# A bias table built by eight matmuls instead of one, an ordering edge in the last block, and two groups side by side in a decoder layer

## The chip, the cores and the metric

The kernel runs on one core of one Trainium2 chip. The metric is the time of one execution on the device in microseconds (us), as the median of several runs. Beside the runs there is one execution taken by the hardware profiler; its span is the time from its first to its last instruction. In the rows of the profile PE is the matrix engine (PEld its weight loads), DVE the vector engine, ACT the scalar engine, POOL the GpSimd engine and SP the engine whose queue starts nearly all transfers; a q behind a name (SPq, ACTq) is that engine's queue of instructions. L430 is line 430 of the kernel.

## The reference

One decoder layer over 2048 positions of width 1024, in float32:

```python
h = rmsnorm(x, norm1[l])
q, k, v, b_gate, c_gate, hc, p = jnp.split(h @ w_in[l], splits, axis=-1)
attn_out = sliding_window_attention(q, k, v, sinks[l], rel_bias)   # 8 heads, window 128
conv_out = short_conv_mixer(b_gate, c_gate, hc, conv_w[l])
pool_out = multiscale_pool_mixer(p, pool_w[l], pool_scale[l])
x = x + jnp.concatenate([attn_out, conv_out, pool_out], -1) @ w_out[l]
x = x + jnp.square(jax.nn.relu(rmsnorm(x, norm2[l]) @ w1[l])) @ w2[l]
return rmsnorm(x, final_norm)
```

In the attention each block of 128 queries sees 256 keys, and to each score a bias is added that depends on the distance between query and key (through 32 buckets) and on the head; outside the window the score is -1e30. For one head the bias of a block is therefore a matrix of 128 by 256 whose rows are one row of 384 values, shifted by one place from row to row.

## The kernel before

Every float32 operand is split into a high part (a cast to the matrix engine's fp32r) and a low part (the rest), and a product is three matmuls of 128 x 128 by 128 x 512: high by high, high by low, low by high (`mm3`, L261 to L264). ACT makes the high part of each weight tile, POOL or DVE the low part (`w_split`, L240 and L241); weights arrive in half tiles of 256 KB through a ring of six buffers (`w_load`, L185) and are split five half tiles ahead of their use (`w_next`).

The work has four stages. Positions are cut into four blocks of 512 (b = 0 to 3); for each block the input projection, the mixers and the output projection are computed. Then the first half of the MLP runs in two passes over 1024 positions each (p = 0 and 1), each in 16 groups (q) of a 2 x 2 block product done with seven products instead of eight (`mlp1`); and then the second half of the MLP.

The program is traced in Python order, and a scheduler of the framework then orders each engine's instructions: program order is the priority, and an instruction whose inputs are ready, by the scheduler's own estimate of times, may be issued ahead of an earlier one that isn't. The order on each engine and queue is then fixed, and each waits at the head of its queue until its inputs are there. `tc.issue_after(ins)` is a context that adds ordering edges: what is traced inside it on the engine of `ins` is queued behind `ins`. The second MLP half already uses it (L1193 to L1196), with an instruction of SP, one of ACT and one of DVE.

Three places matter here.

**The bias table** (`build_bias`, L419 to L433). The one-hot rows (`oh`, 128 x 384) and the bucket values of the heads (`rl`, 128 x 8) are loaded by SP; one matmul in float32 (L427; the profile shows it as two) gives 8 rows of 384 values, one for each head, in 8 partitions; ACT copies them to `e` (L429); one transfer writes each row 128 times to DRAM (`esc`, 8 x 128 x 384 values, 1536 KB, L430); and one transfer reads it back with a row step of 383 instead of 384, so that each row lands shifted by one place (`bias`, 1024 KB, L433). `bias` is first used by the first scores (L559). In the same queue stand the exchanges between the two halves of the partitions of K (`Kd<-Kd`, L511) and Q (`q<-ql`, L543), without which the first scores' matmuls (`sc`, L555) can't start.

**The side work of the last block.** While the last block's input projection runs, `first_rows` (L767) and `first_blocks` (L775) prepare the MLP's input for p = 0: loads of `xb`, 16 scalings (L787) and 16 subtractions (L741) on DVE, and 28 stores, all started by SP. They are called in L862 to L868, after each projection tile.

**The start of pass two.** `norm2_take` (L935) loads one of the seven operand blocks of p = 1 (four transfers of 256 KB), casts it on ACT (L942) and makes the low part on DVE and POOL (L943). Each block has one buffer, so the one for p = 1 can be filled once the last group of p = 0 has used it. The seven calls stand behind the seven products of group 15 of p = 0 (L1020). The transfers land in tiles of the ring `um` (18 buffers of 128 x 512), which also holds the eight intermediate tiles of every group.

Of the kernel before, what the change touches and what calls it, by code (L numbers as in the profile page):

```python
# [69 lines left out]

NEARLY = 5

LAST_DVE = range(28, 44, 2)

NKEEP = NQ - RING
# [7 lines left out]
def tile_trunk(  # L83
# [28 lines left out]
    def plan_load(src):  # L112
        raw_src.append(src)
        return len(raw_src) - 1

    def halves(t):
        return t[:, : HC * P], t[:, HC * P :]
# [4 lines left out]
    N1 = len(plan)  # L122
    ssum, on_dve = {}, {N1 - N1 // NB + i for i in LAST_DVE}

    def plan_group(p, q):

        a = dict(zip(("A11", "A12", "A21", "A22"), halves(w1[2 * q]) + halves(w1[2 * q + 1])))
        on_dve.update(len(plan) + i for i in ON_DVE[p])
        if p == 0:
            at = {n: plan_load(a[n]) for n in ("A11", "A21", "A22", "A12")}  # L130
            at["last"] = WITH[OPS[-1]]
            for o in OPS:
                if WITH[o][0] == "S":
                    ssum[q, WITH[o]] = dr.tile([P, HC * P], F32, name=f"ss_{q}_{o}")
                plan.append((at, (q, WITH[o])))
        else:
            for o in OPS:
                n = WITH[o]
                plan.append((plan_load(a[n] if n[0] == "A" else ssum[q, n]), None))

    def plan_second(q, n):

# [11 lines left out]
        plan.append((r, (op, ssum.get((q, "2" + n)))))  # L154

    for p in range(NP):
        for q in range(NQ):
            plan_group(p, q)
    N2 = len(plan)
    for o in OPS2:  # L160
        for q in range(NQ):
# [99 lines left out]
    def mm3(ps, hi, lo, xh, xl, first, last):  # L261
        pe.matmul(ps, hi, xh, start=first, stop=False)  # L262
        pe.matmul(ps, hi, xl, start=False, stop=False)  # L263
        pe.matmul(ps, lo, xh, start=False, stop=last)  # L264


    prm = cst.tile([P, NPAR], F32, name="prm")
# [21 lines left out]
    def tmp(name):  # L289
        return pB.tile([P, T], F32, tag="tmp", name=name, bufs=4)  # L290
# [103 lines left out]
        dve.tensor_tensor(out=xl[:, k], in0=hf, in1=f32(xh[:, k]), op=ALU.subtract)  # L394


    dve.memset(ones, 1.0 / D)
    warm = cst.tile([P, 1], F32, name="warm")
    act.dma_start(prm, par)
    act.activation(warm, ones, AF.Exp)  # L400
    for k in range(KC):
        norm_load(0, k)
        if k in (0, 2, 4):
            w_load()
            if k < 4:
                w_load()
    make_identity(nc, ident)
    for k in range(KC + 2):
        if k < KC:
# [2 lines left out]
            w_split(dve)  # L412
        if k >= 2:
            norm_square(0, k - 2, gp)


    bias = pA.tile([P, NH, 2 * P], F32, name="bias")

    def build_bias():  # L419
        oh = pA.tile([P, ELEN], F32, tag="pth", name="oh", bufs=3)  # L420
        rl = pA.tile([P, NH], F32, name="rl")
        gp.memset(oh, 0.0)
        gp.memset(rl, 1.0)
        sp.dma_start(oh[0 : NBUCKET + 1], oneh)
        sp.dma_start(rl[0:NBUCKET], rel)
        ps = ps_tr.tile([P, T], F32, tag="tr", name="pse")
        pe.matmul(ps[:NH, :ELEN], rl, oh, start=True, stop=True)  # L427
        e = tmp("e8")
        act.copy(e[:NH, :ELEN], ps[:NH, :ELEN])  # L429
        sp.dma_start(esc[:], e[:NH, :ELEN].unsqueeze(1).to_broadcast([NH, P, ELEN]))  # L430
        full = esc[:]
        skew = bass.AP(full.tensor, full.offset + P - 1, [[ELEN - 1, P], [P * ELEN, NH], [1, 2 * P]])
        sp.dma_start(bias, skew)  # L433


    pwh = pA.tile([P, 2, P], F32R, name="pwh")
# [10 lines left out]
    def build_pw():  # L447
        act.copy(pwh, pwr)
        dve.tensor_tensor(out=pwl, in0=pwr, in1=f32(pwh), op=ALU.subtract)
# [11 lines left out]

    first = {}

    def start_first(tiles):

        ws = [(w_next(0), w_next(0)) for _ in tiles]
        xh, xl = xhl[0]
        pss = [ps_mm.tile([P, T], F32, tag="mm", name=f"pj0_{i}") for i in tiles]
        for step in range(KC + 2 * len(tiles) - 2):
            for n, (w, ps) in enumerate(zip(ws, pss)):  # L470
                k = step - 2 * n
                if 0 <= k < KC:
                    hi, lo = w[k // HC]
                    mm3(ps, hi[:, k % HC], lo[:, k % HC], xh[:, k], xl[:, k], k == 0, k == KC - 1)
        first.update(zip(tiles, pss))

    def proj(b, i, mid=None, bank=None):
        if b == 0 and i in first:
            ps = first[i]
            flush()  # L480
        else:
            xh, xl = xhl[b]
            ps = ps_mm.tile([P, T], F32, tag="mm", name=f"pj{b}_{i}") if bank is None else bank
            for k in range(KC):
                if k % HC == 0:
                    hi, lo = w_next()
                if k == HC and mid:
                    mid()
                mm3(ps, hi[:, k % HC], lo[:, k % HC], xh[:, k], xl[:, k], k == 0, k == KC - 1)
        return ps  # L490

    def scaled(b, i, ps):
# [326 lines left out]
    for b in range(NB):  # L819
        if b == 0:  # L820
            start_first(IN_ORDER[:3])
            load_pw()
            norm_rstd(0)
            build_bias()
            bank = ps_sc.tile([P, 2, T], F32, tag="sc", name="pj0_q")
            first[IN_ORDER[3]] = proj(0, IN_ORDER[3], bank=bank[:, 0])
            norm_bcast(0)
            build_pw()
        for i in IN_ORDER[:NPRE]:
            ps = proj(b, i)  # L830
            evac[i](b, scaled(b, i, ps))
# [3 lines left out]
        for n, i in enumerate(IN_ORDER[NPRE:]):  # L835
            if n < KC and b + 1 < NB:
                norm_load(b + 1, n)

            def mid(n=n):
                if 2 <= n < 10:  # L840
                    st2[n] = att_trans(*st1.pop(n - 2))

            ps = proj(b, i, mid)
            if b and n == 1:
                norm2_row(b - 1, ps_tr, "tr", tmp(f"row2_{b}"))
            if 2 <= n < 10:
                av = att_av(*st2.pop(n))
            evac[i](b, scaled(b, i, ps))
            if 2 <= n < 10:
                att_out(*av, dve if n > 5 else gp)  # L850
            if n < 8:
                st1[n] = att_scores(b, *units[n])
            if n == 5:
                do_pool(b, 0)
            elif n == 7:
                do_pool(b, 1)
                do_pmix(b, 0)
            elif n == 9:
                do_pmix(b, 1)
            if 2 <= n < 4 and b + 1 < NB:  # L860
                norm_square(b + 1, n - 2, gp)
            if b + 1 == NB:  # L862
                if n == 0:
                    first_rows()
                for k, at in enumerate(FIRST):
                    for step in range(3):
                        if n == at[step]:
                            first_blocks(k, step)  # L868
        if b + 1 == NB:
            sA.close()  # L870
            pH, sH = opened("pH", bufs=1, side="right")
# [36 lines left out]
    def um(name):  # L908
        return pT.tile([P, TH], F32, tag="u", name=name, bufs=18)
# [33 lines left out]
            (gp if k == 3 else dve).tensor_tensor(out=lo[:, k], in0=t, in1=f32(hi[:, k]), op=ALU.subtract)  # L943


    def mlp1(p, q, hook):

        def prod(o):
            hi, lo = w_next()
            xh, xl = hbs[p, o]  # L950
            b = bank(f"b{o}_{p}_{q}")
            for k in range(HC):
                mm3(b, hi[:, k], lo[:, k], xh[:, k], xl[:, k], k == 0, k == HC - 1)
            return b

        def put(o, t):
            late.append(lambda: sp.dma_start(hop[o, q][:, p], t))

        def square(out, t, src):
            act.activation(t, src, AF.Relu)  # L960
            act.activation(out, t, AF.Square)

        h11, u, h22, h21, s1, s2, s3, s4 = [
            um(f"{n}_{p}_{q}") for n in ("h11", "u", "h22", "h21", "s1", "s2", "s3", "s4")
        ]
        b = prod("B11")
        act.copy(h11, b)
        hook(0)
        b = prod("T2")
        add(u, h11, b)  # L970
        hook(1)
        b = prod("B21")
        add(h11, h11, b)
        square(h11, h11, h11)
        put("B11", h11)
        hook(2)
        b = prod("T3")
        add(h21, u, b)
        hook(3)
        b = prod("T1")  # L980
        add(h22, h21, b)
        add(u, u, b)
        square(h22, h22, h22)
        put("B22", h22)
        hook(4)
        b = prod("T4")
        add(h21, h21, b)
        square(h21, h21, h21)
        put("B21", h21)
        hook(5)  # L990
        b = prod("B22")
        add(u, u, b)
        h12 = psh.tile([P, TH], F32, tag="h", name=f"h12_{p}_{q}")
        square(h12, u, u)
        sub(s1, h12, h11)
        put("T1", s1)
        sub(s3, h22, h12)
        put("T3", s3)
        sub(s2, h22, s1)
        put("T2", s2)  # L1000
        sub(s4, h21, s2)
        put("T4", s4)
        hook(6)

    ev = {}

# [10 lines left out]
        on((0, 4 + 2 * k, 4), norm2_blocks, 1, k, 1)  # L1017
        on((0, 5 + 2 * k, 1), norm2_blocks, 1, k, 2)
    for i, o in enumerate(OPS):
        on((0, NQ - 1, i), norm2_take, 1, o)  # L1020

    def run(key):
        for f in ev.get(key, ()):
            f()

    for p in range(NP):
        for q in range(NQ):
            mlp1(p, q, lambda i: run((p, q, i)))
    flush()
    for st in (sT, sI, sH):  # L1030
        st.close()
# [253 lines left out]
```

## Time and profile before

| | |
|---|---|
| median of 3 runs | 1968.51 us (1968.17 to 1969.39) |
| the profiled execution, its own time | 1970.88 us |
| span of the profiled execution | 1969.1 us |
| mean granted clock of the matrix engine | 0.982 |
| PE busy | 1887.4 us (96%) |
| DVE, POOL, ACT busy | 1128.1, 1020.5, 893.0 us |
| bytes moved by DMA | 373.34 MB |

The profiled execution's own time is 1.8 us above its span and 2.4 us above the median of the runs. PE is busy almost throughout, so time is lost where PE waits or where its clock is lowered. The first MLP half begins at 670 us and the second at 1317 us (first matmuls into `bB` and into `o`).

### The profile page before, as it was taken

How to read it: one execution, taken by the hardware profiler on the slowest of the kernel's cores; microseconds unless marked ns; L12 is line 12 of the kernel's file. 1: busy time of each engine (PE TensorE's matmuls, PEld its weight loads, DVE VectorE, ACT ScalarE, POOL GpSimd, SP SyncE). 2: the span in 40 equal slices, each digit the busy share in tenths (PEclk: the TensorE clock that was granted, in tenths of full speed). 3: DMA queues.
4: the chain of work that ended last, by engine and by line, in shares of the span. 5: the costliest groups of instructions: out<-in, count | busy, mean ns of one | idle time of the engine just before them, and what ended most of it. 6: DMA issues, size and time to landing. Idle time of an engine off the chain costs nothing. (4 is left out here: it accounts for less than half of the span.)

```text
span 1969.1 us, 25588 instructions
## 1 busy us (share of the span) xinstructions
PE 1887.4 (96%) x8493; PEld 1527.3 (78%) x8493; DVE 1128.1 (57%) x1423; ACT 893.0 (45%) x1633; POOL 1020.5 (52%) x748
## 2 busy tenths in 40 slices
PE   7499999999899999999989999999999999999997
PEld 5377787887687778888868888888888888888887
DVE  6286676676879577765574444443525253642465
ACT  5264575565357354555465454542323222224332
POOL 5275575575554655655454444433565666526521
PEclk9699999999899999999999999999999999999998
DMA  6524624624853779765576555578777666645344
GB/s 203 114 68 148 179 72 136 187 71 124 273 196 125 243 251 326 262 223 197 197 278 193 190 185 190 185 245 295 235 233 235 199 210 213 217 128 168 98 155 134
DMA packets 194016, 373.34 MB, mean 190 GB/s; under 512 B 22047, under 2 KB 30300, under 8 KB 193884
## 3 DMA queue, kind: packets, MB, share of 16 engines
q1 hardware_dynamic: 193740, 371.68, 58.9%
q8 instruction: 67, 1.10, 0.2%
q14 instruction: 65, 0.53, 0.1%
q10 hardware_dynamic: 144, 0.04, 0.0%
HBM read 248.41 MB, written 116.93 MB: 186 GB/s over the span
## 5 line engine op out<-in xcount | busy, mean ns | idle before, releaser
L241 POOL TENSOR_TENSOR wl<-wr,wh 128x512 fp32r<-128x512 f32 x354 | 501.2, 1422 | 509.8 <-ACT wh L240 464.4
L240 ACT CAST wh<-wr 128x512 fp32r<-128x512 f32 x416 | 254.2, 618 | 403.0 <-PE pj L263 79.0
L741 DVE TENSOR_TENSOR bl<-br,bh 128x1024 fp32r<-128x1024 f32 (+2 forms) x144 | 185.3, 1289 | 326.1 <-ACT bh L1081 325.4
L263 PE MATMUL o<-bl,wh 128*128 128x512 f32 (+1 forms) x960 | 363.3, 381 | 0.0
L264 PE MATMUL o<-bh,wl 128*128 128x512 f32 (+1 forms) x960 | 362.7, 381 | 0.0
L262 PE MATMUL o<-bh,wh 128*128 128x512 f32 (+1 forms) x960 | 351.0, 381 | 0.0
L263 PEld LDWEIGHTS o<-bl,wh 128*128 128x128 f32 x960 | 180.8, 188 | 38.3 <-DVE bl L741 0.2
L264 PEld LDWEIGHTS o<-bh,wl 128*128 128x128 f32 x960 | 180.8, 188 | 38.2
L263 PE MATMUL bT<-hlT,wh 128*128 128x512 f32 x512 | 205.0, 400 | 4.1 <-DVE hlT L943 4.1
L262 PEld LDWEIGHTS o<-bh,wh 128*128 128x128 f32 x960 | 176.3, 188 | 38.1
L264 PE MATMUL bT<-hhT,wl 128*128 128x512 f32 x512 | 204.6, 400 | 0.0
L262 PE MATMUL bT<-hhT,wh 128*128 128x512 f32 x512 | 204.5, 400 | 0.0
L262 PE MATMUL pj<-xh,wh 128*128 128x512 f32 x440 | 176.7, 403 | 10.5 <-ACT wh L240 6.8
L263 PE MATMUL pj<-xl,wh 128*128 128x512 f32 x440 | 178.3, 405 | 7.9 <-DVE xl L394 6.2
L264 PE MATMUL pj<-xh,wl 128*128 128x512 f32 x440 | 176.1, 400 | 0.3 <-DVE wl L241 0.3
L241 POOL TENSOR_TENSOR wl<-s,wh 128x512 fp32r<-128x512 f32 x64 | 91.3, 1426 | 141.5 <-ACT wh L240 128.3
L262 PE MATMUL bB<-hhB,wh 128*128 128x512 f32 x384 | 152.1, 397 | 2.6 <-ACT hhB L942 2.6
L263 PE MATMUL bB<-hlB,wh 128*128 128x512 f32 x384 | 152.6, 397 | 0.8 <-DVE hlB L943 0.7
L240 ACT CAST wh<-s 128x512 fp32r<-128x512 f32 x64 | 39.7, 621 | 250.2 <-PE o L263 250.2
L1081 ACT CAST bh<-br 128x1024 fp32r<-128x1024 f32 (+2 forms) x144 | 123.3, 857 | 64.5 <-PE o L264 59.7
L264 PE MATMUL bB<-hhB,wl 128*128 128x512 f32 x384 | 152.1, 396 | 0.0
L208 POOL TENSOR_TENSOR s<-wr,wr 128x512 f32<-128x512 f32 x64 | 127.8, 1997 | 14.5 <-DMA wr<-in_w_dram 9.8
(188 smaller groups left out, 3378.8 us busy)
## 6 DMA issues: line engine op xcount, KB each, us to landing
wr<-in_w_dram SPq DMA_DIRECT2D x256, 256.0 KB, 3.9
hop_T<-s SPq DMA_DIRECT2D x128, 256.0 KB, 2.7
wr<-in_win_dram SPq DMA_DIRECT2D x112, 256.0 KB, 4.2
hop_B<-h SPq DMA_DIRECT2D x96, 256.0 KB, 3.4
br<-hop_B SPq DMA_DIRECT2D x48, 512.0 KB, 4.6
br<-hop_T SPq DMA_DIRECT2D x48, 512.0 KB, 5.0
wr<-in_wout_dram SPq DMA_DIRECT2D x64, 256.0 KB, 2.7
wr<-ss_T SPq DMA_DIRECT2D x48, 256.0 KB, 2.7
```

What stands on the lines that cost most here:

```text
L208: gp.tensor_tensor(out=t, in0=a, in1=b, op=op)
L240: act.copy(hi, src)
L241: eng.tensor_tensor(out=lo, in0=src, in1=f32(hi), op=ALU.subtract)
L262: pe.matmul(ps, hi, xh, start=first, stop=False)
L263: pe.matmul(ps, hi, xl, start=False, stop=False)
L264: pe.matmul(ps, lo, xh, start=False, stop=last)
L741: return dve.tensor_tensor(out=out, in0=a, in1=b, op=ALU.subtract)
L1081: mark["act"] = act.copy(hi, src)
```

## The change

1. The bias: the loads of `oh` and `rl` are started by ACT's queue near the start of the program (`load_bias`) instead of SP's. `build_bias` now runs one float32 matmul per head whose stationary operand is that head's column of `rl` repeated 128 times, so that the row appears in all 128 partitions; ACT copies it (128 x 384) to a tile `e` of the ring `tmp` (four buffers), and SP writes it to `esc[h]` (192 KB). The shifted read is moved into `skew_bias`, called after `norm_bcast(0)` and `build_pw()`.
2. `mm3` returns its last matmul, `proj` keeps it in `latest`, and the calls of `first_rows` and `first_blocks` in the last block stand inside `tc.issue_after(latest[0].ins)`.
3. `mlp1` becomes a generator that stops after each of its seven products. In pass two the groups 0 and 1 are run in turns, product by product; their weights are planned in that order. Four of the seven `norm2_take` calls stand behind products 0, 2, 4 and 6 of the last group of p = 0, the other three behind products 0, 1 and 2 of group 0 of p = 1. The `um` tiles of a group are now taken when they are first needed.

```diff
+NTAKE = 4
@@ plan
+    def groups(p):
+        return [[0, 1]] + [[q] for q in range(2, NQ)] if p else [[q] for q in range(NQ)]
+    def plan_group(p, qs):
+        if p:
+            for i, o in enumerate(OPS):
+                for q in qs:
+                    ...
+                    plan.append((plan_load(a[n] if n in a else ssum[q, n]), None))
+            return
@@ mm3
-        pe.matmul(ps, lo, xh, start=False, stop=last)
+        return pe.matmul(ps, lo, xh, start=False, stop=last)
@@ bias
+    def load_bias():
+        gp.memset(oh, 0.0)
+        gp.memset(rl, 1.0)
+        act.dma_start(oh[0 : NBUCKET + 1], oneh)
+        act.dma_start(rl[0:NBUCKET], rel)
+    def build_bias():
+        for h in range(NH):
+            ps = ps_tr.tile([P, T], F32, tag="tr", name=f"pse{h}")
+            pe.matmul(ps[:, :ELEN], rl[:, h : h + 1].to_broadcast([P, P]), oh, start=True, stop=True)
+            e = tmp(f"e{h}")[:, :ELEN]
+            act.copy(e, ps[:, :ELEN])
+            sp.dma_start(esc[h], e)
+    def skew_bias():
+        full = esc[:]
+        skew = bass.AP(full.tensor, full.offset + P - 1, [[ELEN - 1, P], [P * ELEN, NH], [1, 2 * P]])
+        sp.dma_start(bias, skew)
-        sp.dma_start(oh[0 : NBUCKET + 1], oneh)
-        sp.dma_start(rl[0:NBUCKET], rel)
-        pe.matmul(ps[:NH, :ELEN], rl, oh, start=True, stop=True)
-        act.copy(e[:NH, :ELEN], ps[:NH, :ELEN])
-        sp.dma_start(esc[:], e[:NH, :ELEN].unsqueeze(1).to_broadcast([NH, P, ELEN]))
@@ proj
-                mm3(ps, hi[:, k % HC], ...)
+                latest[0] = mm3(ps, hi[:, k % HC], ...)
@@ block 0
             build_pw()
+            skew_bias()
@@ last block
-                if n == 0:
-                    first_rows()
-                ...
+                with tc.issue_after(latest[0].ins):
+                    if n == 0:
+                        first_rows()
+                    ...
+                                first_blocks(k, step)
@@ pass two
-        on((0, NQ - 1, i), norm2_take, 1, o)
+        on((0, NQ - 1, min(2 * i, 6)) if i < NTAKE else (1, 0, i - NTAKE), norm2_take, 1, o)
...
-        for q in range(NQ):
-            mlp1(p, q, lambda i: run((p, q, i)))
+        for qs in groups(p):
+            tiles = [mlp1(p, q) for q in qs]
+            for i in range(len(OPS)):
+                for q, t in zip(qs, tiles):
+                    next(t)
+                    run((p, q, i))
```

More of the change, by code (lines that the diff above doesn't have):

```diff
@@ L123, in tile_trunk @@
     ssum, on_dve = {}, {N1 - N1 // NB + i for i in LAST_DVE}
-    def plan_group(p, q):
+    def groups(p):
[4 more added lines that the diff above has]
+                for q in qs:
+                    n = WITH[o]
+                    a = {"A11": w1[2 * q][:, : HC * P], "A12": w1[2 * q][:, HC * P :],
+                         "A21": w1[2 * q + 1][:, : HC * P], "A22": w1[2 * q + 1][:, HC * P :]}
+                    if i in ON_DVE[p]:
+                        on_dve.add(len(plan))
+                    plan.append((plan_load(a[n] if n in a else ssum[q, n]), None))
+            return
+        q = qs[0]
         a = dict(zip(("A11", "A12", "A21", "A22"), halves(w1[2 * q]) + halves(w1[2 * q + 1])))
         on_dve.update(len(plan) + i for i in ON_DVE[p])
[L129 to L139, printed above, removed]
+        at = {n: plan_load(a[n]) for n in ("A11", "A21", "A22", "A12")}
+        at["last"] = WITH[OPS[-1]]
+        for o in OPS:
+            if WITH[o][0] == "S":
+                ssum[q, WITH[o]] = dr.tile([P, HC * P], F32, name=f"ss_{q}_{o}")
+            plan.append((at, (q, WITH[o])))
     def plan_second(q, n):
@@ L156, in tile_trunk @@
     for p in range(NP):
-        for q in range(NQ):
-            plan_group(p, q)
+        for qs in groups(p):
+            plan_group(p, qs)
     N2 = len(plan)
@@ L394, in norm_apply @@
         dve.tensor_tensor(out=xl[:, k], in0=hf, in1=f32(xh[:, k]), op=ALU.subtract)
+    bias = pA.tile([P, NH, 2 * P], F32, name="bias")
+    oh = pA.tile([P, ELEN], F32, tag="pth", name="oh", bufs=3)
+    rl = pA.tile([P, NH], F32, name="rl")
+    def load_bias():
[14 more added lines that the diff above has]
+        sp.dma_start(bias, skew)
     dve.memset(ones, 1.0 / D)
@@ L406, in tile_trunk @@
                 w_load()
+    load_bias()
     make_identity(nc, ident)
@@ L414, in tile_trunk @@
             norm_square(0, k - 2, gp)
[L417 to L423, printed above, removed]
-        sp.dma_start(oh[0 : NBUCKET + 1], oneh)
-        sp.dma_start(rl[0:NBUCKET], rel)
[L426 to L433, printed above, removed]
     pwh = pA.tile([P, 2, P], F32R, name="pwh")
@@ L462, in tile_trunk @@
     first = {}
+    latest = [None]
     def start_first(tiles):
@@ L488, in proj @@
                     mid()
-                mm3(ps, hi[:, k % HC], lo[:, k % HC], xh[:, k], xl[:, k], k == 0, k == KC - 1)
+                latest[0] = mm3(ps, hi[:, k % HC], lo[:, k % HC], xh[:, k], xl[:, k], k == 0, k == KC - 1)
         return ps
@@ L862, in tile_trunk @@
             if b + 1 == NB:
-                if n == 0:
-                    first_rows()
[L865 to L868, printed above, removed]
+                with tc.issue_after(latest[0].ins):
+                    if n == 0:
+                        first_rows()
+                    for k, at in enumerate(FIRST):
+                        for step in range(3):
+                            if n == at[step]:
+                                first_blocks(k, step)
         if b + 1 == NB:
@@ L943, in norm2_take, with mlp1 @@
             (gp if k == 3 else dve).tensor_tensor(out=lo[:, k], in0=t, in1=f32(hi[:, k]), op=ALU.subtract)
-    def mlp1(p, q, hook):
+    def mlp1(p, q):
         def prod(o):
@@ L961, in square @@
             act.activation(out, t, AF.Square)
-        h11, u, h22, h21, s1, s2, s3, s4 = [
-            um(f"{n}_{p}_{q}") for n in ("h11", "u", "h22", "h21", "s1", "s2", "s3", "s4")
-        ]
+        h11 = um(f"h11_{p}_{q}")
         b = prod("B11")
         act.copy(h11, b)
-        hook(0)
+        yield
         b = prod("T2")
+        u = um(f"u_{p}_{q}")
         add(u, h11, b)
-        hook(1)
+        yield
         b = prod("B21")
@@ L975, in mlp1 @@
         put("B11", h11)
-        hook(2)
+        yield
         b = prod("T3")
+        h21 = um(f"h21_{p}_{q}")
         add(h21, u, b)
-        hook(3)
+        yield
         b = prod("T1")
+        h22 = um(f"h22_{p}_{q}")
         add(h22, h21, b)
@@ L984, in mlp1 @@
         put("B22", h22)
-        hook(4)
+        yield
         b = prod("T4")
@@ L989, in mlp1 @@
         put("B21", h21)
-        hook(5)
+        yield
         b = prod("B22")
         add(u, u, b)
+        s1, s2, s3, s4 = [um(f"{n}_{p}_{q}") for n in ("s1", "s2", "s3", "s4")]
         h12 = psh.tile([P, TH], F32, tag="h", name=f"h12_{p}_{q}")
@@ L1002, in mlp1 @@
         put("T4", s4)
-        hook(6)
+        yield
     ev = {}
@@ L1026, in tile_trunk @@
     for p in range(NP):
-        for q in range(NQ):
-            mlp1(p, q, lambda i: run((p, q, i)))
+        for qs in groups(p):
+            tiles = [mlp1(p, q) for q in qs]
[3 more added lines that the diff above has]
+                    run((p, q, i))
     flush()
```

## The prediction

> **What bounds the kernel now.** First the page: engine totals and the slices.
>
> ```profile
> span 1969.1 us, 25588 instructions
> PE 1887.4 (96%) x8493; PEld 1527.3 (78%) x8493; DVE 1128.1 (57%) x1423; ACT 893.0 (45%) x1633; POOL 1020.5 (52%) x748
> ...
> PE   7499999999899999999989999999999999999997
> ...
> PEclk9699999999899999999999999999999999999998
> ```
>
> PE is the bound; no other engine passes 57%. A change can only win where PE stands still or its clock is lowered: the second slice (49 to 98 us) is the only one far below 9, the eleventh (492 to 541 us) and the twenty-first (985 to 1034 us) dip in PE or clock. Second view, PE's waits, longest first:
>
> ```profile
> PE sc L555 <- DMA q<-ql: 29.9, 3, 27.4
> ...
> PE pj L263 <- DVE xl L394: 6.2, 6, 2.6
> PE bT L263 <- DVE hlT L943: 4.1, 3, 1.9
> ...
> PE bB L262 <- ACT hhB L942: 2.6, 1, 2.6
> ```
>
> One wait of 27.4 us outweighs everything; the next are those of the last block's beginning (`xl`) and of pass two's beginning (`hlT`, `hhB`). Third, the windows around these three places, with a dense one as measure (columns: length, busy time and number of instructions of PE, PEld, DVE, ACT, POOL; granted clock; share of DMA; GB/s):
>
> ```profile
> 49.00:76.30 27.30, 0.00 (x0) 0.00 (x0) 0.85 (x2) 0.52 (x2) 0.19 (x1) 0.56 0.63 128
> 76.30:83.00 6.70, 6.64 (x20) 5.50 (x21) 2.08 (x3) 1.46 (x6) 3.98 (x5) 0.51 0.44 129
> 500.00:517.00 17.00, 11.61 (x34) 7.37 (x33) 17.00 (x18) 7.27 (x14) 10.34 (x7) 0.70 0.81 258
> ...
> 1000.00:1024.00 24.00, 17.31 (x60) 12.63 (x59) 18.06 (x22) 15.34 (x28) 15.61 (x10) 0.86 0.73 260
> 1040.00:1060.00 20.00, 20.00 (x87) 16.10 (x86) 8.90 (x12) 10.18 (x17) 8.52 (x7) 1.00 0.57 187
> ```
>
> The dense window gives 20/87 = 0.230 us for a matmul. So 500 to 517 holds 34 matmuls where 74 fit: 9.2 us lost. 1000 to 1024 holds 60 where 104 fit: 10.2 us lost, 6.7 as waits (24 - 17.31) and 3.5 as slow clock. After the long stall the clock stays at half until 83: 20 matmuls (eight half-empty `sc`, some 0.8 us, and twelve full, 2.8 us, if fast) take 6.7 us, so 3.1 us more are lost.
>
> **Part 1, the bias.** The wait names `q<-ql`, but Q's low parts are ready by 45.6. The queue of SP shows who held them:
>
> ```profile
> 31.76 0.82 SPq L430 DMA_DIRECT2D esc<-e  x1
> 35.92 6.85 SPq L185 DMA_DIRECT2D wr<-in_win_dram  x1
> 65.60 0.38 SPq L433 DMA_DIRECT2D bias<-esc  x1
> ...
> 66.70 1.42 SPq L511 DMA_DIRECT2D Kd<-Kd  x2
> 68.22 2.10 SPq L543 DMA_DIRECT2D q<-ql  x2
> ```
>
> ```profile
> SPq L433 <- DMA esc<-e: 22.8, 1, 22.8
> ```
>
> The shifted read waits at the head of SP's queue until the write of `esc` has landed, 33.8 us after its issue (31.76 to 65.60), and K's and Q's exchanges stand behind it. Why is that write so slow? The DMA view of the stretch 45 to 55 us, where it is alone, and then of 30 to 35 us:
>
> ```profile
> DMA packets 325, 0.50 MB, mean 50 GB/s; under 512 B 0, under 2 KB 325, under 8 KB 325
> ...
> q1 hardware_dynamic: 325, 0.50, 44.2%
> ```
>
> ```profile
> DMA packets 957, 1.74 MB, mean 348 GB/s; under 512 B 107, under 2 KB 142, under 8 KB 956
> ```
>
> Eight partitions feed it at 50 GB/s and 44% of the engines' time, some 7 of 16; five us of mixed loads move seven times as much. After the change each of eight stores reads 128 partitions, as the stores of `hop` do:
>
> ```profile
> hop_T<-s SPq DMA_DIRECT2D x128, 256.0 KB, 2.7
> ...
> q<-ql SPq DMA_DIRECT2D x32, 128.0 KB, 5.3
> ```
>
> A store of 192 KB should land in 2.7 us or less; eight, issued as the copies end, are down some 10 us after the first instead of 33.8. `bias` is read before Q is ready, and its own landing lies beside projections. So the 27.4 us stall goes, and with it the slow clock: 30.5 us.
>
> What it costs (the present matmul pair with its successor, and the copy):
>
> ```profile
> 30.26 0.81 PE L427 MATMUL pse<-oh,rl 128*8 128x384 f32 x2
> 31.00 0.51 PE L262 MATMUL pj_q<-xh,wh 128*128 128x512 f32 x1
> ```
>
> ```profile
> 31.11 0.47 ACT L429 COPY e<-pse 8x384 f32<-8x384 f32 x1
> ```
>
> A pair takes 0.74 us of PE (30.26 to 31.00), and 128 output partitions instead of 8 stream the same 384 columns: seven more are 5.2 us if they run in program order on a busy PE. PE's gaps before the stall:
>
> ```profile
> 6.80:29.40 22.60, 20.64 (x73) 14.01 (x74) 18.14 (x15) 13.67 (x26) 18.40 (x12) 1.00 0.76 255
> 29.40:48.97 19.57, 18.17 (x87) 14.32 (x85) 11.44 (x25) 10.40 (x18) 5.48 (x4) 1.00 0.63 144
> ```
>
> They hold 2.0 + 1.4 = 3.4 us, so the cost is between 1.8 and 5.2 us. The scheduler does fill gaps with later work (POOL copies the sinks of the first scores at 5.22 us, 70 us before their use), and `oh` now arrives early:
>
> ```profile
> 5.22 0.32 POOL L558 COPY s<-prm 128x4 f32<-128x4 f32 x2 [3.21 <-DMA prm<-in_par_dram]
> ```
>
> I take 2.7. ACT's seven more copies, 3.3 us, lie in its 9.2 idle us of 29.40 to 48.97; without that cover they would delay Q's casts by as much. SP's seven more issues, at the 0.38 us of the shifted read's (2.7 us), lie in the 6.85 us in which its queue waits for a weight buffer anyway; uncovered they would delay Q's exchange. The two loads moved to ACT's queue cost it as much each, ahead of its first real work, and leave SP's queue:
>
> ```profile
> 5.01 0.63 ACT L358 ACTIVATE acc<-xr 128x512 f32<-128x512 f32 x1 [2.35 <-DMA xr<-in_xT_dram]
> ```
>
> ACT stood idle before it; without that cover they would add 0.8 us to the start.
>
> What is late next is Q's exchange itself. Its time from the last low part to the first scores, here and in the last block:
>
> ```profile
> 43.87 1.72 DVE L539 TENSOR_TENSOR ql<-z,q 64x512 fp32r<-64x512 f32 x2
> ```
>
> ```profile
> 535.08 0.70 DVE L539 TENSOR_TENSOR ql<-pj,q 64x512 fp32r<-64x512 f32 x1
> ```
>
> ```profile
> 538.70 0.36 PE L555 MATMUL sc<-Kd,q 128*128 128x256 f32 x1 [2.13 <-DMA q<-ql]
> ```
>
> In the last block it is 538.70 - 535.78 = 2.9 us. Here Q's low part is ready at 45.59, so scores could start at 48.5, just when PE arrives at 49: no wait. With the median landing of 5.3 us and an issue of 0.5, it is 51.4: 2.4 us. I take 1.0, as the read of `bias` runs near it. Net of part 1: 27.4 + 3.1 - 2.7 - 1.0 = 26.8 us.
>
> [...]
>
> **Part 2, the last block.** The 9.2 us at 500 to 517 us are DVE's, and part of them is this side work:
>
> ```profile
> 497.78 0.75 DVE L787 SCALAR_TENSOR_TENSOR xb<-xb,prm,rb_acc 128x512 f32<-128x512 f32 x1 [6.10 <-DMA xb<-x1s]
> ```
>
> A scaling of `xb` stood at the head of DVE's queue for 6.1 us, waiting for its load, with the `xl` of the new block behind it; then DVE is busy without a break (17.00 of 17). The change would queue such work behind each tile's last matmul. But the edge goes only to instructions on the engine of the instruction named. That is a PE matmul, and the block wrapped contains transfers on SP's queue and DVE arithmetic, none on PE. So I expect no edge at all, and 0 us. If it acted: a gain of up to 9.2 us, or, as the ends bound it, a loss of like size, should 32 DVE instructions (at this row's 0.75 us, 24 us) be pushed into the scores' stretch.
>
> **Part 3, pass two.** Seven operand blocks, 7 MB, are wanted one every 12 matmuls (2.76 us), and the last shows how late:
>
> ```profile
> 1005.59 1.84 SPq L941 DMA_DIRECT2D xu_B<-x2s_B  x4
> ```
>
> ```profile
> 1018.56 2.17 ACT L942 CAST hhB<-xu_B 128x512 fp32r<-128x512 f32 x4
> ```
>
> ```profile
> xu_B<-x2s_B SPq DMA_DIRECT2D x16, 256.0 KB, 5.9
> ```
>
> Side by side, each block serves 24 matmuls, 5.5 us. Pass two starts near 995 us, three products (8.3 us) before this first wait of its fourth:
>
> ```profile
> 1003.51 0.50 PE L263 MATMUL bT<-hlT,wh 128*128 128x512 f32 x1 [0.81 <-DVE hlT L943]
> ```
>
> A take needs 1.8 us of issues, 5.9 of landing and about 2.7 of casts (2.17) and the last subtraction: 10.4. T1, hooked 2.8 us after the start, is ready at 13.2 and due after eight products at 22.1; T4 at 18.7, due 27.6; B22 at 24.2, due 33.1: 8.9 us to spare each. The four takes in the last group of p = 0, hooked 5.5 us apart from 978.4, are ready at 988.8, 994.3, 999.9 and 1005.4, due at 995, 1000.5, 1006 and 1011.6: 6 us to spare. So all 10.2 us go. Matmuls, loads and evacuations keep their number; two groups hold 16 of 18 `um` tiles at their end, where a short wait of DVE or ACT is covered by seven PSUM banks of 2.76 us each; without that cover the end of the pair would cost PE a landing, 2.7 us.
>
> The three waits of 0.8 to 1.9 us and one of 2.6 are followed by 3.5 us of slow clock, so the window's row gives 10.2. [...]
>
> **Sum.** 26.8 + 0 + 10.2 = 37.0 us: 1970.9 to 1933.9 us for the profiled execution. The median of the runs is 2.4 us lower: 1968.5 - 37.0 = 1931.5 us.
>
> **Rivals.**
> - *The ordering acts after all*, or the new schedule happens to spare the last block: 9.2 us more, 1922.3. For it: the loss is there to be had. Against: no instruction it could bind.
> - *Each DMA engine keeps its slow pace* (50 GB/s over 7 engines, 7.1 each, against 22 in the mixed stretch). Sixteen then carry 114 GB/s and the 1536 KB take 13.8 us; 20.0 of the 33.8 go, a stall of 7.4 us and the slow clock stay, the extra matmuls hide in it: 1968.5 - 20.0 - 10.2 = 1938.3. Against it: the `hop` store, 256 KB in 2.7 us with its latency.
> - *Pass two still waits*, because the pair's tiles leave too few of the 18 `um` buffers to land the takes: 10.2 us given back, 1941.7. For it: with eight of the last group, T3's four and one of the new group, T1's four make 17. Against: stores free them in 2.7 us, and 9 us are to spare.
> - *Slower:* the eight stores run one after another, each held up in SP's queue behind loads that wait, with the four `tmp` tiles and PE's order behind them. At 0.47 + 0.38 + the 6.8 us that `bias` took to land, they need 61 us, 27 more than now: 1968.5 + 27 - 10.2 = 1985. It decides from (33.8 + 10.2)/8 = 5.5 us a head.
>
> ```profile
> bias<-esc SPq DMA_DIRECT2D x1, 1024.0 KB, 6.8
> ```
>
> **How the numbers follow.** Forecast 62%, ordering acts 10%, slow pace 12%, pass two waits 10%, slower 4%, anything else 2%. The forecast's own terms move it from 1924 (no residual wait, matmuls in gaps, and some luck in the last block) to 1937 (5.2 and 2.4 us, and a clock drop after the wait). The range 1919 to 1946 takes in the first four cases. A measurement here tells 0.2%, 3.9 us, from no change: faster 0.94, same 0.01, slower 0.05.
>
> **What would show it.** Part 1: eight `esc` stores landing in about 3 us, PE's wait for `q<-ql` in the first block under 3 us, and a granted clock of 1.00 at 60 to 80 us. Part 2: a DVE wait for `xb<-x1s` still ahead of the last block's `xl`, some 34 matmuls in the 17 us after its start. Part 3: no PE wait on `hlT` or `hhB`, two groups' `bB` in turns. I am wrong if SP's queue holds `q<-ql` behind `bias<-esc` again, if PE waits on `pse`'s copies, or if the last block changes much.

## The result, and the profile after

The changed kernel takes 1938.55 us (median; 1935.74 to 1940.97), the kernel before 1968.57 us beside it: a ratio of 0.9847, 95% interval 0.9829 to 0.9864. That is 30.0 us less, where 37.0 were forecast; 1938.55 lies inside the range of 1919 to 1946. The profiled execution took 1936.93 us, 33.95 less than that of before. Its page, with the same rows as shown of before:

```profile
span 1935.2 us, 25620 instructions
PE 1892.6 (98%) x8507; PEld 1527.8 (79%) x8507; DVE 1123.6 (58%) x1423; ACT 895.9 (46%) x1640; POOL 1020.0 (53%) x748
...
PE   8999999999899999999999999999999999999997
...
PEclk9999999999899999999999999999999999999998
```

The second slice is now full; the eleventh still dips; the twenty-first doesn't. PE's waits show the same (total, times, longest):

```profile
PE pj L275 <- DVE xl L406: 5.8, 7, 2.9
PE sc L577 <- DMA q<-ql: 3.6, 5, 2.2
...
PE bB L275 <- DVE hlB L967: 0.7, 1, 0.7
```

Of 29.9 us for `q<-ql` 3.6 are left, `xl` keeps 5.8 of 6.2, and of pass two's waits there is 0.7. Four windows of the changed kernel, the stall's old place first, then block 0's end, the first 26 us of the last block, and pass two's beginning:

```profile
49.00:76.30 27.30, 26.23 (x136) 21.44 (x135) 18.76 (x25) 16.64 (x44) 16.41 (x16) 1.00 0.47 128
120.00:140.00 20.00, 17.52 (x65) 12.09 (x66) 17.22 (x28) 11.80 (x20) 6.30 (x8) 0.83 0.14 39
479.10:505.10 26.00, 20.47 (x80) 14.96 (x78) 25.94 (x27) 8.99 (x16) 16.25 (x10) 0.87 0.82 257
975.00:1000.00 25.00, 25.00 (x108) 19.92 (x107) 19.65 (x24) 15.25 (x29) 14.91 (x10) 1.00 0.88 310
```

Where the time went is read from the starts of four matmuls in both traces: the first score, block 0's first output projection, the first of each MLP half. Before:

```profile
76.36 0.45 PE L555 MATMUL sc<-Kd,q 128*128 128x128 f32 x1 [27.39 <-DMA q<-ql]
...
142.97 0.48 PE L262 MATMUL po<-mxh,wh 128*128 128x512 f32 x1
...
670.48 0.40 PE L262 MATMUL bB<-hhB,wh 128*128 128x512 f32 x1
...
1317.33 0.87 PE L262 MATMUL o<-bh,wh 128*128 128x512 f32 x3
```

After:

```profile
52.38 0.30 PE L577 MATMUL sc<-Kd,q 128*128 128x128 f32 x1 [0.31 <-DMA q<-ql]
...
117.56 0.48 PE L274 MATMUL po<-mxh,wh 128*128 128x512 f32 x1
...
648.33 0.40 PE L274 MATMUL bB<-hhB,wh 128*128 128x512 f32 x1
...
1283.28 0.86 PE L274 MATMUL o<-bh,wh 128*128 128x512 f32 x3
```

| reached | after is ahead by | gained in this stretch | forecast |
|---|---|---|---|
| first score | 24.0 us | 24.0 | 23.7 to 24.7 |
| block 0's output projection | 25.4 | 1.4 | 3.1 of slow clock, less what is left of the 1.0 |
| first MLP half | 22.2 | -3.2 | 0 |
| second MLP half | 34.0 | 11.8 | 10.2 |
| end (1969.1, 1935.2) | 33.9 | -0.1 | 0 |

The first and the fourth rows carry the change. The third is a loss that no step of the prediction had: 3.2 us in a stretch whose work the change leaves alone, but for part 2 in its last 170 us. The experiments go mostly to that row.

### The profile page after: what moved, and what is told of

It reads as the page before. It is cut to its first block, busy times and chain, and to the rows that moved or that the text cites. A ratio compares the mean times of both kernels' runs of the same rounds, so it can differ in the third digit from the quotient of the medians.

```text
span 1935.2 us, 25620 instructions
## 1 busy us (share of the span) xinstructions
PE 1892.6 (98%) x8507; PEld 1527.8 (79%) x8507; DVE 1123.6 (58%) x1423; ACT 895.9 (46%) x1640; POOL 1020.0 (53%) x748
## 4 chain that ended last, share of the span: by engine, by line
PE 83%; DVE 7%; DMA 6%; issue 2%; ACT 1%; POOL 1%; SPq 1%; DVEq 0%; POOLq 0%; ACTq 0%
PE o L274 11%; PE o L275 11%; PE o L276 11%; PE bT L275 6%; PE bT L276 6%; PE bT L274 6%; PE bB L275 5%; PE bB L274 5%; PE bB L276 5%; PE pj L275 4%; PE pj L276 4%; PE pj L274 4%; DMA x1s<-xo 1%; PE pt L604 1%; DVE xl L406 1%
## 5 line engine op out<-in xcount | busy, mean ns | idle before, releaser
L220 POOL TENSOR_TENSOR s<-wr,wr 128x512 f32<-128x512 f32 x64 | 128.5, 2008 | 14.9 <-DMA wr<-in_w_dram 10.2
```

Of the source, the lines that this page charges most:

```text
L220: gp.tensor_tensor(out=t, in0=a, in1=b, op=op)
```

## The experiments

Each kernel was timed against the kernel before on the same chip.

**Parts 1 and 3 alone.** `bias_only` is the kernel before with all edits of the bias; `pair_only` is the kernel before with the generator `mlp1`, `groups` and the moved takes. Neither has the `issue_after`.

```diff
bias_only: before, and
+    load_bias()              # ACT's queue, at the start
+    build_bias()             # eight matmuls, copies and stores
+    skew_bias()              # after build_pw()

pair_only: before, and
+        for qs in groups(p):
+            tiles = [mlp1(p, q) for q in qs]
             ...
```

> The kernel before with part 1 of the change alone (eight matmuls for the bias rows, loads on ACT's queue, shifted read later). Theory A: what the changed kernel has gained when its MLP begins, 22 us: 1946 us; the projection spacing is 235 ns, since part 1 is what moves xh and xl. Rival, by the prediction's term for part 1 without any loss by address: 1968.5 - 26.8 = 1941.7 us. Rival that the ordering edge of part 2 did save something in the last block: a last block worse here than in the changed kernel by some us, so above 1949 us.

> The kernel before with part 3 of the change alone (two groups side by side, takes spread). Theory A: all that is lost at the start of pass two goes, by the landmarks of the two traces 11.8 us: 1956.7 us; projection spacing 231 ns. The prediction's term: 10.2 us, 1958.3 us. Rival that the side-by-side pair leaves a wait: above 1962 us.

`bias_only`: 1948.72 us, ratio 0.9892 (0.9876 to 0.9908), 21.3 us under the 1970 that its ratio implies. `pair_only`: 1957.67 us, ratio 0.9936 (0.9923 to 0.9950), 12.6 us. The two make 33.9, the whole change 30.1 and 30.7 in two measurements, reckoned the same way; each of these numbers is uncertain by some 3 us, so they add as far as that can be told. `bias_only` lies between its theory A (1946) and the rival that part 2 had saved something (above 1949), so the traces have to decide. The first 26 us of the last block in `bias_only`, which has no ordering, the same place in the kernel before, and the place of pass two's wait in `pair_only`:

```profile
482.20:508.20 26.00, 21.04 (x80) 15.64 (x78) 25.94 (x27) 8.35 (x15) 15.40 (x10) 0.87 0.82 252
```

```profile
501.20:527.20 26.00, 20.61 (x73) 14.77 (x72) 25.94 (x27) 9.28 (x17) 16.25 (x11) 0.80 0.82 254
```

```profile
990.00:1014.00 24.00, 23.76 (x102) 18.83 (x101) 17.89 (x23) 15.95 (x30) 14.51 (x10) 1.00 0.81 284
```

80 matmuls at a clock of 0.87 stand in that stretch of `bias_only` as in the changed kernel, with and without part 2. The kernel before has 73, at 0.80; but `pair_only`, which lacks part 2 as well, has 84 at 0.87 (501.6 to 527.6 us), so this difference isn't part 2's. And the program compiled from the kernel before with part 2 alone (not run) has the same instructions in the same order on every engine as the kernel before: the edge binds nothing. In `pair_only` pass two is dense.

**The ordering made to act.** In `order_engines` the same side work is ordered behind the last DVE and the last SP instruction instead of a PE one, on the changed kernel. `after_again` is the changed kernel beside it.

```diff
-                with tc.issue_after(latest[0].ins):
+                with ExitStack() as order:
+                    for e in (dve, sp):
+                        order.enter_context(tc.issue_after(last_of(e)))
```

> The changed kernel with the last block's side work queued behind the last instruction traced so far on DVE and on SP, instead of behind a matmul of PE. Theory A (part 2 did nothing because it named an instruction of PE, and the side work is what holds up the last block's beginning): PE's waits on xl at that place (5.8 us) and the slow clock behind them go, 8.5 us, of which up to 3 us may come back where the scalings and subtractions now stand between the scores: 1930 to 1933 us against 1938.5. Rival (DVE has too much to do there in any order): the loss only moves into the scores' stretch, 1938 us or more.

> The changed kernel once more, beside the next kernels on the same chip: ratio 0.985 to that of before. Its last block loses 8 to 9 us at its beginning in each execution, as in the first profile.

`order_engines`: 1938.06 us, ratio 0.9838 (0.9825 to 0.9852). `after_again`: 1938.80 us, ratio 0.9844 (0.9831 to 0.9858). No difference can be told, so the rival (1938 us or more) holds and not theory A (1930 to 1933). Two windows of each tell why: the last block from its first projection to its first output projection, and from there to the first MLP half. First `after_again`, then `order_engines`:

```profile
483.00:601.50 118.50, 107.19 (x509) 86.10 (x508) 102.53 (x133) 64.57 (x151) 65.41 (x51) 0.96 0.59 190
601.50:650.20 48.70, 47.27 (x203) 37.56 (x202) 37.63 (x46) 28.10 (x51) 23.91 (x16) 1.00 0.76 251
```

```profile
479.70:591.30 111.60, 103.28 (x497) 83.55 (x495) 88.45 (x117) 61.97 (x147) 67.38 (x49) 0.98 0.61 188
591.30:649.30 58.00, 52.58 (x212) 40.13 (x213) 48.04 (x59) 30.67 (x53) 24.55 (x17) 0.94 0.73 249
```

With a working order the first stretch is 6.9 us shorter and the second 9.3 us longer: DVE's 14 us of work (102.53 to 88.45) come back as 10.4 (37.63 to 48.04) when the output projection needs DVE too, and PE's idle time and slow clock come with them: in the second stretch PE's waits for DVE grow from 1.4 to 5.2 us. So the place of this work wasn't what cost the time: in both places tried, PE waits for DVE. Over the two stretches the working order loses 2.4 us. That its MLP starts at 649.3 us and not later than the other's 650.2 is due to a lead of 3.3 us that it had before the last block began (479.7 against 483.0), where the two programs do the same work.

**The bias store with one matmul.** Theory P: what made the old store slow is that its eight source rows lie side by side in eight partitions, not that there are eight. `spread_rows` is the kernel before with the rows in partitions 0, 18, ... 126; still one matmul, one copy, one store with an outermost dimension of eight.

```diff
+        rs = pA.tile([P, P], F32, name="rs")
+        gp.memset(rs, 1.0)
+        gp.tensor_copy(rs[:, 0 : 18 * NH - 17 : 18], rl)
-        pe.matmul(ps[:NH, :ELEN], rl, oh, start=True, stop=True)
+        pe.matmul(ps[:, :ELEN], rs, oh, start=True, stop=True)
-        sp.dma_start(esc[:], e[:NH, :ELEN].unsqueeze(1).to_broadcast([NH, P, ELEN]))
+        sp.dma_start(esc[:], e[0 : 18 * NH - 17 : 18, :ELEN].unsqueeze(1).to_broadcast([NH, P, ELEN]))
```

> The kernel before, still with one matmul pair and one write of esc, but the eight heads' rows stand in partitions 0, 18, 36 ... 126 instead of 0 to 7. Theory P (the write was slow because its eight source rows lie side by side in SBUF): the write lands in under 12 us instead of 33.8, the stall goes, and without the seven extra matmul pairs: 1968.5 - 30 + 1 = 1939.5 us. Theory E (it was slow because only eight rows feed it, each at its own pace of 7 GB/s): 33.8 us as before, 1968.5 us. [...]

1947.73 us, ratio 0.9888 (0.9874 to 0.9901): as much as `bias_only`. SP's queue, the DMA view of 36 to 40 us, and the first score with PE's wait for Q:

```profile
32.09 0.82 SPq L433 DMA_DIRECT2D esc<-e  x1
...
44.22 0.38 SPq L436 DMA_DIRECT2D bias<-esc  x1
...
46.89 1.83 SPq L546 DMA_DIRECT2D q<-ql  x2
```

```profile
DMA packets 607, 0.95 MB, mean 238 GB/s; under 512 B 11, under 2 KB 535, under 8 KB 607
```

```profile
55.34 0.45 PE L558 MATMUL sc<-Kd,q 128*128 128x128 f32 x1 [6.25 <-DMA q<-ql]
```

The shifted read is started 12.1 us after the store instead of 33.8. The 1.5 KB packets of the store (512 B to 2 KB) run at 535 - 11 = 524 in 4 us, 131 per us, against 325 in 10 us, 32.5 per us, before: four times the pace, again from eight rows. Theory P holds. Why a store from eight neighbouring partitions is slow, these runs do not show. The time stays 8 us above the 1939.5 expected: PE reaches the scores at 49.1 us and then waits for Q's exchange, which was issued at 46.89, 8.5 us ahead of the first score. In the changed kernel (its rows stand below) it is issued at 45.64, 6.7 us ahead of the first score, but PE, with the extra matmuls to do, comes at 52.07 and waits 0.3. So the extra matmuls lie in time that `spread_rows` waits. That the 1024 KB read of `bias`, started 1.1 us ahead of K's exchange, slows the exchange is likely, and not shown: from 44 to 56 us the DMA engines are busy for 0.93 of the time in both traces.

**The address of the projections' operand.** In the compiled programs `xh` and `xl` start at byte 134016 and 150400 of each partition before, multiples of 128, and at 148384 and 164768 after, 32 beyond such a multiple, since part 1 allocates `bias`, `oh` and `rl` ahead of them. The weights of the some 1300 matmuls of the input projections start at 64 mod 128 in both. 49 of them in a row, undisturbed, in block 1 (first and last start; 48 steps), before and after:

```profile
207.71 0.39 PE L264 MATMUL pj<-xh,wl 128*128 128x512 f32 x1
...
218.69 0.39 PE L264 MATMUL pj<-xh,wl 128*128 128x512 f32 x1
```

```profile
183.07 0.39 PE L276 MATMUL pj<-xh,wl 128*128 128x512 f32 x1
...
194.28 0.40 PE L276 MATMUL pj<-xh,wl 128*128 128x512 f32 x1
```

10.98/48 = 229 ns before, 11.21/48 = 233 to 234 ns after. `x_aligned` puts 32 unused bytes ahead of `xh` in the changed kernel, so that it starts at a multiple of 128 again; `x_shifted` puts the same 32 bytes into the kernel before, so that it lies 96 beyond one. The order of instructions stays what it was in each.

```diff
     pwl = pA.tile([P, 2, P], F32R, name="pwl")
+    pad = pA.tile([P, 8], F32, name="pad")
```

> The changed kernel with an unused tile of 32 bytes behind xl; every engine's order is the same, but xr, xh and xl start at a multiple of 64 bytes, as they did before the change. Theory A (the 32-byte shift of xh and xl slows the input projection): start-to-start time of the projection's matmuls falls from 235 to 231 ns, 1344 of them give 5 us, so 1933.5 us against the 1938.5 of the change. Rival B (the spacing comes from the new order or from the missing pause, not from the address): 1938.5 us, spacing 235 ns.

> The kernel before with the same unused tile of 32 bytes, which here moves xh and xl off a multiple of 64 bytes; the order is that of before. Theory A: 1968.5 + 5 = 1973.6 us, projection spacing 235 ns. Rival B: 1968.5 us and 231 ns.

(The spacings of these expectations are means over all neighbouring pairs, 2 ns above those of undisturbed rows.) The same 48 steps in `x_aligned` and in `x_shifted`:

```profile
184.09 0.39 PE L276 MATMUL pj<-xh,wl 128*128 128x512 f32 x1
...
195.08 0.39 PE L276 MATMUL pj<-xh,wl 128*128 128x512 f32 x1
```

```profile
207.40 0.39 PE L264 MATMUL pj<-xh,wl 128*128 128x512 f32 x1
...
218.59 0.40 PE L264 MATMUL pj<-xh,wl 128*128 128x512 f32 x1
```

10.99 us and 11.19 us, 229 and 233 ns: the spacing follows the address both ways, with no instruction changed. The time follows less: `x_aligned` 1936.17 us, ratio 0.9829 (0.9815 to 0.9842), 2.4 us under the changed kernel, 3.5 by the ratios, with intervals that overlap, so that no gain is shown; `x_shifted` 1971.73 us, ratio 1.0010 (1.0001 to 1.0019), 2 us over the kernel before, where 5 were expected. In its trace PE is busy for 509.0 us between block 0's output projection and the MLP, 2.8 us longer than before, and idle for 3.0 us less, so the stretch is as long as before (527.3 and 527.5 us): slower matmuls took the place of waits.

**All operands.** The MLP's operands lie badly in both kernels: `hh`, `hl`, `bh`, `bl`, `mxh` and `mxl` at 96 beyond a multiple of 128, the weights at 64. `all_aligned` moves `xh`, `xl`, `mxh` and `mxl` of the changed kernel to multiples of 128 and the MLP's moving operands to 64 mod 128; `aligned_128` moves these to multiples of 128 too; `aligned_128w` also the weights; `before_128w` does all of it to the kernel before. Only unused bytes are added, so the order of instructions stays; small tiles allocated behind them move along.

```diff
+    cst.tile([P, 16], F32, name="padC")            # weights; in the two kernels with w
+    pB.tile([P, 24], F32, name="padB")             # mxh; [P, 8] where padC is left out
+            pA.tile([P, 8], F32, name="padA")      # xh; not in before_128w
+    pH.tile([P, 24], F32, name="padH")             # hh, hl; [P, 8] in all_aligned
+    pG.tile([P, 24], F32, name="padG")             # bh, bl; [P, 8] in all_aligned
```

> The changed kernel with four unused tiles of 32 bytes, so that the moving operands of nearly all matmuls start at a multiple of 64 bytes (xh, xl and mxh, mxl at a multiple of 128 too, the MLP's hh, hl, bh, bl not); orders unchanged. Theory A (64 bytes matter): spacing in the MLP falls from 234.4 to 231 ns, 5568 matmuls give 19 us, the four blocks some 4 us more (there DVE takes back a part): 1915 us. Rival (only a multiple of 128 helps): the MLP's spacing stays at 234.4 ns, 1933 us.

> The same program as all_aligned, on the chip of the two beside it, as their measure: 1926 us, MLP spacing 232.5 ns, by either theory.

> As all_aligned, but the unused tiles ahead of the MLP's operands (hh/hl in the first product, bh/bl in the second) are 96 bytes instead of 32, so that these operands lie at multiples of 128 bytes instead of 64 mod 128. Theory M (only the moving operand's address sets the spacing: a multiple of 128 gives 231 ns, 64 mod 128 gives 232.5, 32 or 96 mod 128 gives 234.4): the MLP's matmuls stand 231 ns apart, 1.5 ns less for some 5600 of them, 8 us: 1918 us. Theory N (232.5 ns in the MLP has another cause, such as its weights' addresses or its loads): spacing and time stay, 1926 us.

> As aligned_128, and 64 unused bytes ahead of the weights' pools put all weights (wh, wl) at multiples of 128 bytes instead of 64 mod 128; mxh and mxl stay at multiples of 128. Theory M (the weights' addresses do not matter; the input projection stood at 231 ns with weights at 64 mod 128): the same as aligned_128. Theory W (the stationary operand's address counts as well): 1.5 ns less for the MLP's 5600 matmuls or for all 8500 than aligned_128, 8 to 13 us below it.

> The kernel before with unused bytes alone: 64 ahead of the weights' pools, 96 ahead of mxh, and 96 each ahead of the MLP's two sets of moving operands, so that all weights, xh/xl, mxh/mxl, hh/hl and bh/bl lie at multiples of 128 bytes as in aligned_128w; the instructions and their order are those of the kernel before. Theory A+ (the addresses' worth adds to the change's): aligned_128w stands some 37 us under the changed kernel, of which 2 to 5 are the input projection's, which the kernel before has nearly right already, so 32 to 35 us here: 1934 to 1937 us, spacing 227 ns in the MLP. Theory D (much of it is taken up by the waits that the change removed, or by DVE in the blocks): under 27 us, above 1941 us.

| kernel | MLP's moving operands, weights (mod 128) | us | ratio to before |
|---|---|---|---|
| changed | 96, 64 | 1938.55 | 0.9847 (0.9829 to 0.9864) |
| `all_aligned` | 64, 64 | 1926.08 | 0.9792 (0.9772 to 0.9812) |
| `all_aligned_again` | 64, 64 | 1928.72 | 0.9795 (0.9779 to 0.9810) |
| `aligned_128` | 0, 64 | 1910.63 | 0.9695 (0.9681 to 0.9709) |
| `aligned_128w` | 0, 0 | 1901.08 | 0.9644 (0.9631 to 0.9657) |
| `before_128w` | 0, 0 | 1932.80 | 0.9813 (0.9799 to 0.9826) |

The same 500 us of the second MLP half, in the changed kernel, `all_aligned_again`, `aligned_128`, `aligned_128w` and `before_128w` (the third number is that of PE's matmuls):

```profile
1300.00:1800.00 500.00, 500.00 (x2136) 402.04 (x2135) 203.83 (x133) 157.21 (x209) 281.96 (x172) 1.00 0.68 213
```

```profile
1300.00:1800.00 500.00, 500.00 (x2154) 405.69 (x2153) 203.76 (x133) 159.09 (x212) 287.92 (x176) 1.00 0.68 212
```

```profile
1300.00:1800.00 500.00, 500.00 (x2186) 410.27 (x2185) 212.51 (x143) 161.25 (x218) 295.98 (x179) 1.00 0.67 208
```

```profile
1300.00:1800.00 500.00, 500.00 (x2211) 414.34 (x2210) 215.21 (x158) 161.43 (x218) 294.60 (x179) 1.00 0.66 207
```

```profile
1300.00:1800.00 500.00, 500.00 (x2208) 414.15 (x2207) 213.90 (x141) 162.87 (x217) 288.76 (x175) 1.00 0.71 222
```

PE is 100% busy at full clock in all five; yet 2136, 2154, 2186, 2211 and 2208 matmuls stand in them: 234.1, 232.1, 228.7, 226.1 and 226.4 ns each. (The kernel before has 2136 as well.) `all_aligned` came out between its two theories, 1915 and 1933 us, so neither held. Theory M was right that the moving operand counts and wrong that it alone does and in its sizes: from 64 to 0 mod 128 brought 3.4 ns, not 1.5, and 18 us instead of 8. Theory W was right of the weights: 2.6 ns and 9.6 us. Theory N falls. With `before_128w` theory A+ holds, with a little more than it expected: 1932.8 us, 37.1 under the kernel before, and `aligned_128w` is 31.7 under that (33 by the ratios), where the change alone is worth 30. So the layout and the change add up within the noise, and the unused bytes alone are worth more than the whole change. `aligned_128w` is the fastest version found.

## Why the prediction held, and where it missed

**Part 1 up to the first score** came out as forecast, by a way that differs in its terms. The stall was read rightly, and is gone: SP's queue after,

```profile
30.88 0.86 SPq L427 DMA_DIRECT2D esc<-e  x1
...
38.15 2.21 SPq L427 DMA_DIRECT2D esc<-e  x4
43.25 0.37 SPq L432 DMA_DIRECT2D bias<-esc  x1
...
45.64 1.47 SPq L565 DMA_DIRECT2D q<-ql  x2
```

the landing of the eight stores (KB each, median us), and PE's wait for Q between 45 and 60 us:

```profile
esc<-e SPq DMA_DIRECT2D x8, 192.0 KB, 3.2
```

```profile
PE sc L577 <- DMA q<-ql: 1.1, 3, 0.5
```

The shifted read starts 12.4 us after the first store, and 1.1 us of waiting are left where 1.0 was taken. The parts behind that agreement differ: Q's exchange was given 2.9 to 5.8 us from Q's last low part to the first scores, and here 6.7 pass from its issue alone; but PE comes later too, at 52.07 where 49 was read. The extra matmuls weren't mostly hidden: fourteen more of them between the column sums and the broadcast of the norm,

```profile
27.29 0.95 PE L314 MATMUL pst_n<-ones,acc 128*128 128x1 f32 x8
...
35.73 3.77 PE L424 MATMUL pse<-oh,rl 128*128 128x384 f32 x10
39.33 0.83 PE L356 MATMUL pbc_n<-ident,r 128*128 128x128 f32 x6
```

and 12.0 us from `pst_n`'s start to `pbc_n`'s, where before it is

```profile
29.38 0.95 PE L302 MATMUL pst_n<-ones,acc 128*128 128x1 f32 x8
...
36.63 1.05 PE L344 MATMUL pbc_n<-ident,r 128*128 128x128 f32 x8
```

7.2 us. That is 4.8, next to the upper bound of 5.2, where 2.7 was taken. A pair with 128 output partitions takes what the one with 8 took: five fill PE from 35.73 to 39.33, 0.72 us each, against 0.74. But `pst_n` starts 2.1 us earlier, so that the broadcast is late by 2.7 after all. Two of the prediction's edits could have done this (SP's queue relieved of two loads at the start, or the scheduler's new order there); no run separates them, and `pair_only`, which has neither, also starts it 1.1 us earlier than the kernel before. A right sum of wrong terms is luck, not skill. That the rows' place, not their number, made the store slow follows from `spread_rows`: one store of eight rows there too, its outermost dimension eight, and the shifted read starts 12.1 us after it instead of 33.8. The rival that each DMA engine keeps its slow pace is out: the last four stores, 768 KB, went out from 38.15 and were down by 43.25, 154 GB/s beside the weight loads where its estimate, sixteen engines at 7.1 GB/s each, had 114 for all, and no stall of 7.4 us is left. Its total, 1938.3 us, is nevertheless nearer to the 1938.55 measured than the forecast's 1931.5: that is chance, and the time alone would have spoken for the wrong mechanism.

**The slow clock** after the stall: 3.1 us forecast, 1.4 seen. The clock is 1.00 at 49 to 76 us, as forecast; 0.8 of the difference is the rest of Q's wait (0.75 of its 1.1 us fall behind the first score). The other 0.9 wasn't taken apart.

**The stretch to the MLP**, forecast at 0 and measured at -3.2, is the step that failed. The working costed each instruction by its row of before and took for granted that part 1 leaves the blocks behind the first scores as they were. It doesn't: between block 0's output projection and the MLP lie 527.5 us before, 526.8 in `spread_rows` and 527.8 in `pair_only`, which lack part 1, but 530.2 in `bias_only` and 530.8 and 530.6 in two executions of the changed kernel. (Two executions of one program, `all_aligned`, differ by 1.7 here.) So the loss comes with part 1. Its new tiles moved `xh`, and the projections' matmuls went from 229 to 233 ns; but that is not shown to be most of the loss. `x_aligned` takes 528.9 us, but `aligned_128`, whose `xh` lies as well as there, 530.2, and `x_shifted`, whose `xh` lies badly, 527.3. And with all operands at multiples of 128 in both, `before_128w` and then `aligned_128w`,

```profile
141.43 0.71 PE L262 MATMUL po<-mxh,wh 128*128 128x512 f32 x2
...
667.10 0.39 PE L262 MATMUL bB<-hhB,wh 128*128 128x512 f32 x1
```

```profile
118.44 0.71 PE L274 MATMUL po<-mxh,wh 128*128 128x512 f32 x2
...
646.44 0.39 PE L274 MATMUL bB<-hhB,wh 128*128 128x512 f32 x1
```

the stretch takes 525.7 and 528.0 us: in one execution each, 2.3 us are lost all the same. What else in part 1 makes the loss stays open. One thing that varies here is not the change's: the clock at block 0's end, 0.83 in the window of the changed kernel above, is 0.91 in the same window of the same program run again,

```profile
120.00:140.00 20.00, 15.13 (x61) 10.99 (x60) 18.35 (x27) 12.57 (x22) 7.43 (x8) 0.91 0.18 50
```

1.00 in the kernel before in its like, 140 to 160 us, and 0.74 in `pair_only` (143 to 163 us), whose blocks are those of the kernel before. It falls without a long gap: the longest wait of PE between 117.6 and 140 us in the changed kernel is 1.9 us. What lowers it there, no run shows.

**Part 2** did nothing, for the reason given: no edge exists. The last block's 26 us hold 80 matmuls with and without it. The rival that the ordering acts, 9.2 us, would have failed even where it acts, as `order_engines` shows: the loss that the prediction set beside this gain comes as well, in the output projection and not among the scores, and takes all of it.

**Part 3** gained 11.8 us in the changed kernel and 12.6 as a kernel of its own, for 10.2; no wait on `hlT` or `hhB` is left and the clock stays 1.00. That the slow clock is part of it (3.5 of the 10.2) is borne out: the waits alone were 6.7. What the 1.6 us beyond the 10.2 are, no run shows.

**The step from the profiled execution to the median** is the largest miss. The sum gave 1933.9 for the profiled execution, 3.0 under the 1936.9 seen; then 2.4 were taken off because the profiled execution of before stood 2.4 above its median. That of after stands 1.6 below its own. So 4.0 of the 7.1 us between forecast and median come from treating one execution's distance from the median as a constant; the other 3.0 are the 3.2 us of the blocks and the 1.7 of the slow clock, less 1.6 that part 3 gained more, with small change of 0.3.

## What to carry to other kernels

Before a stall is fixed by more work on the bound engine, look at where the rows of the slow transfer lie: one matmul with its rows spread over the partitions did as much as eight (1947.73 and 1948.72 us). A new tile moves the tiles allocated after it, as part 1's moved `xh` from byte 134016 to 148384: compare the addresses of the bound engine's operands before and after, and the spacing of the same undisturbed matmuls in both traces (229 and 233 to 234 ns here); a busy share of 100% at full clock says nothing of it (2136 to 2211 matmuls in 500 us of it here). And where an engine that others wait for is busy for most of a stage, as DVE was here for 102.5 of 118.5 us, ordering may move the wait instead of removing it.

## What the runs showed of the hardware that was not expected

The time of a matmul of 128 x 512 in this format depends on where its operands start in the partition: 226 ns with moving operand and weights at multiples of 128 bytes, 229 with the weights at 64 mod 128, 232 with both at 64, 234 with the moving operand at 96 and the weights at 64. This holds over 500 us each at full clock with no wait; in undisturbed rows of 49 matmuls with the weights at 64 it was 229 ns with the moving operand at 0, and 233 at 32 and at 96. Which of the reads makes the difference, and how, these runs do not show. And a store whose eight source rows lie in neighbouring partitions moved 50 GB/s (32.5 packets of 1.5 KB per us), one whose eight rows lie 18 partitions apart some four times that (131 per us).
